# Modulation vectors of a transformer kernel: products on ScalarE and sums by adding DMAs instead of fused multiply-adds on VectorE

## The chip, the cores and the metric

The kernel runs on one core of one Trainium2 chip. The time is the device time of one execution in microseconds (us); the median of three runs is given. The engines are TensorE (PE, with its weight loads as PEld), VectorE (DVE), ScalarE (ACT), GpSimd (POOL) and SyncE (SP, which only issues DMAs here). An engine works through its own queue in order, and waits at an instruction whose semaphores are not yet there.

## The reference, cut to what matters

Two blocks follow each other on 512 tokens of width 1024. The first has two hybrid layers (sliding-window attention, retention, gated linear attention), the second two layers with other mixers and a feed-forward part. All numbers are float32. The change touches the three modulation vectors that each hybrid layer makes from one conditioning vector `c`:

```python
c_act = jax.nn.silu(c)                       # 1 x 1024
mod = c_act @ w_mod + b_mod                  # w_mod 1024 x 3072, per layer
shift, scale, gate = jnp.split(mod[:, None, :], 3, axis=-1)
h = rms_norm(x, pre_gain) * (1.0 + scale) + shift
...
return x + gate * rms_norm(y, post_gain)
```

So each vector is a product of a row of 1024 numbers with a matrix of 1024 x 1024, plus a row of biases; 4 MB of weights are read for each of the six vectors.

## The kernel before, in words

Activations stay in SBUF. Large products run on PE as three passes of float32r matmuls (`mm3`, L230): weights come in tiles of 128 x 512 (`load_w`, L208), SP loads the raw tile (four buffers), ACT casts the high part (L226), DVE subtracts for the low part (L227), and PE uses both. The work of a layer is a set of Python generators (`dsteps`, L328) that are pulled in turn, so that dense matmul steps fill the gaps of the serial parts: the seven levels of the gated attention's decay matrix (`level_ops`, L696, with DVE, ACT and POOL's L704 in turn, and DVE's masked copies L725), the chain of the gated attention (`gla_chain`, L748), the retention (`ret_chain`, L795), the window attention (`attend`, L890).

Modulation vectors: the first layer's first two are made at the very start by other code (`mod0`, L416, on PE and DVE). The other four are made in the background by `mod_steps(l, i)` (L356): layer 0's gate, then layer 1's scale and shift during layer 0, and layer 1's gate during layer 1 (`bg`, L598). They are pulled in the levels (1.5 steps after each of 14 half levels, L722 and L727), then one step for each step of the other chains. A vector has two halves of 512 columns, and a half has eight steps of 128 rows of weights. A step before the change loads a tile `rawm` (two buffers, SP's queue, L368) and does on DVE `acc = rawm * ca[:, k] + acc` (`mod_acc`, L385 to L390; the first step is a product and an addition of the bias row, L387 and L388). The sum over the 128 partitions is left to a matmul with a tile of ones, which gives every partition the result (L375); this part, `late`, is put off by `RT['mdl']` = 4 steps:

```python
ps = ps_mm()
PE.matmul(ps, ones, src, start=True, stop=True)
if i == 0:
    SC.copy(dst, ps)
elif i == 1:
    V.scalar_tensor_tensor(dst, ps, 1.0, dst, op0=OP.add, op1=OP.mult)
else:
    V.tensor_tensor(dst, ps, dst, op=OP.mult)
```

The tile `acc` has one buffer, so a half can begin only when the matmul of the half before has read it. The gain (512 KB, spread over the partitions) is loaded into the vector's own tile ahead (L360), and the late part multiplies by it in place. `later(steps, fn)` (L309) runs `fn` after that many steps of dense matmuls (`tick`, L312); `flush` (L318, called at L686, L792, L881, L1021 and elsewhere) runs at once whatever is still put off. The code gives a program order; the framework then lays out each engine's queue from it and may draw an instruction forward when its operands are there, and it sets all the waits. The layer's gate is read at L1003 and L1005, the next layer's scale and shift at L400 and L401 (`norm`). `bias_steps` (L1109) follows the last vector and uses the same `rawm` buffers.

Of the kernel before, what the change touches and what calls it, by code (L numbers as in the profile page):

```python
# [9 lines left out]
F32 = mybir.dt.float32  # L10
# [4 lines left out]
OP = mybir.AluOpType  # L15
# [6 lines left out]
D = 1024  # L22
# [22 lines left out]
def _constants():  # L45
# [32 lines left out]
    def put2(name, a):  # L78
# [32 lines left out]
RT = dict(f0=5, f1=4, op1=16, op2=6, Lng=7, Le=5, Lc=5, Ld=6, LA=5, LB=5, Lao=5, Lcbn=10, Ldf9=7, Lln=9, Llnf=13, Lrms=7, Lkk=2, Loc=7, Luq=3, Lod=5, h0=17, h1=10,  # L111
          l0=7, lv=3.3, mdl=4, rm=9, na=3, nb=4, u1=4.6, u2=4.4, u0=2.9, df=0.6, cmp=1.485, lr0=0.4, lr1=0.21, lr2=0.175, lr3=0.085, ml=0.5, gl=2, rt=2, at=1, cb=5)
# [9 lines left out]
def _body(ctx, tc, nc, a, out, stop):  # L122
    V, SC, GP, PE = nc.vector, nc.scalar, nc.gpsimd, nc.tensor

    def pool(name, bufs=1, space=None, stack=ctx, side=None):
        kw = {}
        if space:
            kw["space"] = space
        else:
            kw["reuse_waits"] = "tile"  # L130
        if side:
            kw["side"] = side
        return stack.enter_context(tc.tile_pool(name=name, bufs=bufs, **kw))
# [20 lines left out]
    def ps_mm():  # L154
        return psum("mm", [128, 512], 4)
# [26 lines left out]
    ones = cp.tile([128, 128], F32, name="ones")  # L182
# [101 lines left out]
    def bcast_row(dst, row):  # L284
        n = row.shape[-1]
        nc.sync.dma_start(dst, bass.AP(tensor=row.tensor, offset=row.offset, ap=[[0, 128], [1, n]]))
# [22 lines left out]
    def later(steps, fn, key=None):  # L309
        pend.append((clock[0] + steps, fn, key))  # L310
# [31 lines left out]
    def first_block():  # L342
# [3 lines left out]
        md = pool("md", stack=st)  # L346
        more_w("wb", 4, st, None)
        ca = fp.tile([128, 8], F32, name="ca")
# [5 lines left out]
        mod = [[None] * 3 for _ in range(2)]  # L354

        def mod_steps(l, i):  # L356
            t_ = md.tile([128, D], F32, name=f"mod{i}", bufs=1)
            mod[l][i] = t_
            if i:
                bcast_row(t_, (a["pre_norm_gain"] if i == 1 else a["post_norm_gain"])[l])  # L360
            for n in range(0, D, 512):
                c0 = D * i + n
                acc = md.tile([128, 512], F32, name="acc", bufs=1)
                br = md.tile([128, 512], F32, tag="rawm", name="br", bufs=2)[0:1]
                nc.sync.dma_start(br, a["b_mod"][l:l + 1, c0:c0 + 512])
                for k in range(8):
                    raw = md.tile([128, 512], F32, tag="rawm", name="rawm", bufs=2)
                    nc.sync.dma_start(raw, a["w_mod"][l, 128 * k:128 * k + 128, c0:c0 + 512])  # L368
                    mod_acc(acc, raw, br, k)
                    if k < 7:  # L370
                        yield 1

                def late(dst=t_[:, n:n + 512], src=acc):
                    ps = ps_mm()
                    PE.matmul(ps, ones, src, start=True, stop=True)  # L375
                    if i == 0:
                        SC.copy(dst, ps)
                    elif i == 1:
                        V.scalar_tensor_tensor(dst, ps, 1.0, dst, op0=OP.add, op1=OP.mult)
                    else:  # L380
                        V.tensor_tensor(dst, ps, dst, op=OP.mult)
                later(RT['mdl'], late, "mod")
                yield 1

        def mod_acc(acc, raw, br, k, eng=V):  # L385
            if k == 0:
                eng.tensor_scalar(acc, raw, ca[:, 0:1], None, op0=OP.mult)  # L387
                eng.tensor_tensor(acc[0:1], acc[0:1], br, op=OP.add)  # L388
            else:
                eng.scalar_tensor_tensor(acc, raw, ca[:, k:k + 1], acc, op0=OP.mult, op1=OP.add)  # L390

        def norm(l, t, x, pl):
# [5 lines left out]
            for n in range(2):  # L398
# [5 lines left out]
        sil = ([fp.tile([128, 512], F32, name=f"sil_a{t}") for t in range(4)],  # L404
               [fp.tile([128, 256], F32, name=f"sil_r{t}") for t in range(4)])
        Ks = [dict(mod=mod[l], sil=sil, mod_steps=mod_steps, norm=norm, md=md) for l in range(2)]
        load_E, mm_E, ev_E = start_layer(0, Ks[0])
        nst = ExitStack()
# [3 lines left out]
        gain = np_.tile([128, D], F32, name="gain")  # L412
# [1755 lines left out]
```

## Time and profile before

| | before |
|---|---|
| median of three runs | 1942.95 us (1939.66 to 1948.47) |
| the profiled execution's own time | 1936.26 us |
| its span | 1934.5 us |
| mean granted clock of PE | 0.992 |
| busy: PE, DVE, ACT, POOL | 1874.2, 1251.6, 828.1, 260.1 us |
| read from HBM, written | 207.20 MB, 14.09 MB |

The profile is of one execution. A row of instructions gives the source line, the engine, the operation, output and inputs, and shapes; in square brackets stands how long the engine sat idle before it and what ended that wait. A matmul's length overlaps with its neighbours', so a PE that reads as busy is not always at its peak. SP's and POOL's DMA issues appear as instructions; POOL's have a time of their own, since POOL itself writes the transfer's descriptors.

### The profile page before, as it was taken

How to read it: one execution, taken by the hardware profiler on the slowest of the kernel's cores; microseconds unless marked ns; L12 is line 12 of the kernel's file. 1: busy time of each engine (PE TensorE's matmuls, PEld its weight loads, DVE VectorE, ACT ScalarE, POOL GpSimd, SP SyncE). 2: the span in 40 equal slices, each digit the busy share in tenths (PEclk: the TensorE clock that was granted, in tenths of full speed). 3: DMA queues.
4: the chain of work that ended last, by engine and by line, in shares of the span. 5: the costliest groups of instructions: out<-in, count | busy, mean ns of one | idle time of the engine just before them, and what ended most of it. 6: DMA issues, size and time to landing. Idle time of an engine off the chain costs nothing.

```text
span 1934.5 us, 29305 instructions
## 1 busy us (share of the span) xinstructions
PE 1874.2 (97%) x10144; PEld 1518.6 (79%) x10144; DVE 1251.6 (65%) x3060; ACT 828.1 (43%) x1840; POOL 260.1 (13%) x380
## 2 busy tenths in 40 slices
PE   7899899999999999999999999999999999999997
PEld 4777687877888888868888888788778888888886
DVE  5697886485775244686675674755776776756646
ACT  2432354433463344453443443244665544434341
POOL 3011101012101000101020020101441200200101
PEclk9999999999999999999999999999999999999999
DMA  8535524226124233403373362363114033733632
GB/s 278 173 89 165 150 86 137 86 84 183 44 94 157 73 106 121 153 12 116 117 155 99 91 149 72 117 188 91 42 29 148 24 133 112 154 97 96 134 88 82
DMA packets 139784, 218.76 MB, mean 113 GB/s; under 512 B 21633, under 2 KB 53747, under 8 KB 139636
## 3 DMA queue, kind: packets, MB, share of 16 engines
q1 hardware_dynamic: 130420, 200.11, 33.6%
q0 software_dynamic: 9216, 16.78, 5.2%
q8 instruction: 80, 1.31, 0.3%
q14 instruction: 68, 0.56, 0.1%
HBM read 207.20 MB, written 14.09 MB: 114 GB/s over the span
## 4 chain that ended last, share of the span: by engine, by line
PE 65%; DVE 7%; issue 6%; POOL 3%; DMA 2%; ACT 1%; POOLq 0%; DVEq 0%; SPq 0%; ACTq 0%
PE mm L1060 10%; PE mm L1062 10%; PE mm L1061 9%; PE mm L231 6%; PE mm L233 6%; PE mm L232 6%; PE t L1095 1%; PE o L1547 1%; PE o L1549 1%; PE o L1548 1%; DMA bq<-in_ffn_w_down_dram 1%; PE mm L1547 1%; PE mm L1549 1%; PE mm L1548 1%; PE t L274 1%
## 5 line engine op out<-in xcount | busy, mean ns | idle before, releaser
L227 DVE TENSOR_TENSOR w<-raw,w 128x512 fp32r<-128x512 f32 (+4 forms) x496 | 307.5, 638 | 140.1 <-ACT w L226 138.4
L226 ACT CAST w<-raw 128x512 fp32r<-128x512 f32 (+4 forms) x504 | 284.5, 575 | 239.8 <-PE mm L233 55.9
L1060 PE MATMUL mm<-hT,w 128*128 128x512 f32 x920 | 366.6, 399 | 0.2
L1062 PE MATMUL mm<-hT,w 128*128 128x512 f32 x920 | 361.6, 394 | 0.1
L1061 PE MATMUL mm<-hT,w 128*128 128x512 f32 x920 | 360.7, 392 | 0.0
L231 PE MATMUL mm<-w,hT 128*128 128x512 f32 (+3 forms) x704 | 278.3, 396 | 1.4 <-ACT hT L243 1.3
L233 PE MATMUL mm<-w,hT 128*128 128x512 f32 (+3 forms) x704 | 262.5, 373 | 0.4 <-DVE hT L244 0.4
L232 PE MATMUL mm<-w,hT 128*128 128x512 f32 (+3 forms) x704 | 261.0, 371 | 0.1
L1060 PEld LDWEIGHTS mm<-hT,w 128*128 128x128 f32 x920 | 172.9, 188 | 39.7 <-ACT w L226 1.8
L1062 PEld LDWEIGHTS mm<-hT,w 128*128 128x128 f32 x920 | 172.7, 188 | 39.4 <-DVE w L227 1.3
L1061 PEld LDWEIGHTS mm<-hT,w 128*128 128x128 f32 x920 | 172.9, 188 | 35.2
L231 PEld LDWEIGHTS mm<-w,hT 128*128 128x128 f32 x704 | 138.9, 198 | 31.0 <-issue 6.5
L233 PEld LDWEIGHTS mm<-w,hT 128*128 128x128 f32 x704 | 138.8, 197 | 21.9 <-DVE hT L244 1.3
L232 PEld LDWEIGHTS mm<-w,hT 128*128 128x128 f32 x704 | 139.4, 198 | 16.8 <-issue 2.0
L1525 POOL DMA_DIRECT2D bq<-in_ffn_w_down_dram x64 | 56.6, 1280 | 413.0 <-DVE w L244 401.7
L1576 DVE SCALAR_TENSOR_TENSOR g<-mm,cw,g 128x511 f32<-128x511 f32 x44 | 33.0, 749 | 108.5 <-ACT g L1575 108.4
L243 ACT CAST w<-bq 128x512 fp32r<-128x512 f32 x112 | 69.0, 621 | 65.1 <-DMA bq<-in_ffn_w_down_dram 20.2
L1090 ACT ACTIVATE E<-E,nm 128x128 f32<-128x128 f32 (+3 forms) x128 | 71.6, 560 | 45.0 <-DVE nm L1089 42.3
L244 DVE TENSOR_TENSOR w<-bq,w 128x512 fp32r<-128x512 f32 x112 | 75.5, 689 | 15.4 <-ACT w L243 14.8
L1582 DVE TENSOR_TENSOR ge<-ge,mm 128x512 f32<-128x512 f32 x44 | 30.1, 685 | 67.6 <-PE mm L1062 67.5
L1575 ACT ACTIVATE g<-mm,cw 128x512 f32<-128x512 f32 x44 | 34.2, 777 | 79.6 <-PE mm L1062 63.1
L1085 DVE COPY pT<-t 128x512 f32<-128x512 f32 (+3 forms) x84 | 43.0, 512 | 37.8 <-PE t L1280 23.3
(472 smaller groups left out, 3458.3 us busy)
## 6 DMA issues: line engine op xcount, KB each, us to landing
raw<-in_ffn_w_up_dram SPq DMA_DIRECT2D x160, 256.0 KB
rawm<-in_w_mod_dram SPq DMA_DIRECT2D x96, 256.0 KB
raw<-in_w_in_dram SPq DMA_DIRECT2D x80, 256.0 KB
bq<-in_ffn_w_down_dram POOLq DMA_DIRECT2D x64, 256.0 KB, 7.7
raw<-in_ev_w_in_dram SPq DMA_DIRECT2D x48, 256.0 KB
bq<-in_ffn_w_down_dram SPq DMA_DIRECT2D x48, 256.0 KB
raw<-in_w_out_dram SPq DMA_DIRECT2D x32, 256.0 KB
raw<-in_ffn_w_down_dram SPq DMA_DIRECT2D x24, 256.0 KB
```

Of the source, the lines that this page charges most:

```text
L226: SC.copy(hi, r)
L227: (eng or V).tensor_tensor(lo, r, hi.bitcast(F32), op=OP.subtract)
L231: PE.matmul(ps, hi, w[:, 0, w0:w0 + n], start=first, stop=False)
L232: PE.matmul(ps, hi, w[:, 1, w0:w0 + n], start=False, stop=False)
L233: PE.matmul(ps, lo, w[:, 0, w0:w0 + n], start=False, stop=last)
L243: SC.copy(hi, ps)
L244: V.tensor_tensor(lo, ps, hi.bitcast(F32), op=OP.subtract)
L1060: PE.matmul(ps, wh, hi, start=k == ks[0], stop=False)
L1061: PE.matmul(ps, wh, lo, start=False, stop=False)
L1062: PE.matmul(ps, wl, hi, start=False, stop=k == ks[-1])
L1090: SC.activation(E, E, AF.Exp, scale=scale, bias=nm, accum_out=den)
L1525: GP.dma_start(bufs[name, p], src[then](p), accum_op=OP.add)
```

## The change: products on ACT, sums by DMA, one late part for both halves

The loop over the eight tiles of 128 rows is now the outer one and the two halves the inner one, and a step returns to the caller after the load is issued. ACT then multiplies the raw tile by its column of `c`: for the first row tile into the vector's own tile, else in place. The sum is made by DMAs that add to the vector's own tile: the bias row from HBM (2 KB) and each product tile (256 KB). They are issued from POOL. The separate accumulator is gone; its tile name now holds the gain, half by half, loaded inside the late part. The late part covers both halves and is put off by 16 steps instead of 4.

```diff
             t_ = md.tile([128, D], F32, name=f"mod{i}", bufs=1)
             mod[l][i] = t_
-            if i:
-                bcast_row(t_, (a["pre_norm_gain"] if i == 1 else a["post_norm_gain"])[l])
-            for n in range(0, D, 512):
-                c0 = D * i + n
-                acc = md.tile([128, 512], F32, name="acc", bufs=1)
-                br = md.tile([128, 512], F32, tag="rawm", name="br", bufs=2)[0:1]
-                nc.sync.dma_start(br, a["b_mod"][l:l + 1, c0:c0 + 512])
-                for k in range(8):
+            gain = (None, a["pre_norm_gain"], a["post_norm_gain"])[i]
+            for k in range(8):
+                for n in range(0, D, 512):
+                    c0 = D * i + n
+                    acc = t_[:, n:n + 512]
                     raw = md.tile([128, 512], F32, tag="rawm", name="rawm", bufs=2)
                     nc.sync.dma_start(raw, a["w_mod"][l, 128 * k:128 * k + 128, c0:c0 + 512])
-                    mod_acc(acc, raw, br, k)
-                    if k < 7:
-                        yield 1
-
-                def late(dst=t_[:, n:n + 512], src=acc):
+                    yield 1
+                    if k == 0:
+                        SC.mul(acc, raw, ca[:, 0:1])
+                        GP.dma_start(acc[0:1], a["b_mod"][l:l + 1, c0:c0 + 512], accum_op=OP.add)
+                    else:
+                        SC.mul(raw, raw, ca[:, k:k + 1])
+                        GP.dma_start(acc, raw, accum_op=OP.add)
+
+            def late():
+                for n in range(0, D, 512):
+                    dst = t_[:, n:n + 512]
                     ps = ps_mm()
-                    PE.matmul(ps, ones, src, start=True, stop=True)
+                    PE.matmul(ps, ones, dst, start=True, stop=True)
                     if i == 0:
                         SC.copy(dst, ps)
-                    elif i == 1:
-                        V.scalar_tensor_tensor(dst, ps, 1.0, dst, op0=OP.add, op1=OP.mult)
+                        continue
+                    g = md.tile([128, 512], F32, name="acc", bufs=1)
+                    bcast_row(g, gain[l, n:n + 512])
+                    if i == 1:
+                        V.scalar_tensor_tensor(dst, ps, 1.0, g, op0=OP.add, op1=OP.mult)
                     else:
-                        V.tensor_tensor(dst, ps, dst, op=OP.mult)
-                later(RT['mdl'], late, "mod")
-                yield 1
+                        V.tensor_tensor(dst, ps, g, op=OP.mult)
+            later(16, late, "mod")
+            yield 1
```

`mod0`, `mod_acc` and the rest of the kernel stay as they are.

## Rows read from the trace of the kernel before

**Rows 1.** The page's part 1: busy time, share of the span and instructions of each engine.

```profile
PE 1874.2 (97%) x10144; PEld 1518.6 (79%) x10144; DVE 1251.6 (65%) x3060; ACT 828.1 (43%) x1840; POOL 260.1 (13%) x380
```

**Rows 2.** Stretches: length; PE, PEld, DVE, ACT, POOL busy (count); clock, DMA share, GB/s.

```profile
60.00:330.00 270.00, 250.48 (x1541) 203.97 (x1539) 211.02 (x524) 113.35 (x283) 33.58 (x53) 0.99 0.44 131
...
70.00:230.00 160.00, 147.73 (x964) 118.92 (x963) 128.15 (x303) 54.64 (x128) 27.37 (x40) 0.98 0.48 142
100.00:150.00 50.00, 47.66 (x432) 38.65 (x431) 47.12 (x102) 16.73 (x42) 7.79 (x9) 1.00 0.38 109
...
160.00:170.00 10.00, 7.80 (x25) 5.57 (x24) 6.62 (x18) 0.86 (x2) 1.20 (x2) 0.66 0.22 65
...
420.00:430.00 10.00, 9.11 (x120) 8.04 (x117) 9.13 (x20) 3.55 (x8) 2.28 (x2) 0.80 0.39 107
430.00:440.00 10.00, 10.00 (x53) 6.05 (x53) 6.42 (x12) 4.59 (x9) 0.00 (x0) 0.86 0.53 154
```

**Rows 3.** Timeline 72 to 82: start, length, engine, line, operation, [idle before <- what ended it].

```profile
72.88 0.43 SPq L368 DMA_DIRECT2D rawm<-in_w_mod_dram  x1
...
73.83 1.25 SPq L1112 DMA_DIRECT2D tb<-in_rel_bias_dram  x1
...
76.92 0.49 DVE L387 TENSOR_SCALAR acc<-rawm,ca 128x512 f32<-128x512 f32 x1 [4.14 <-DMA rawm<-in_w_mod_dram]
77.43 4.80 SPq L368 DMA_DIRECT2D rawm<-in_w_mod_dram  x4
...
78.26 0.28 PE L617 MATMUL t<-con,ga 128*16 128x128 f32 x1 [1.85 <-DVE ga L612]
...
80.25 1.63 DVE L390 SCALAR_TENSOR_TENSOR acc<-rawm,ca,acc 128x512 f32<-128x512 f32 x2 [2.05 <-DMA rawm<-in_w_mod_dram]
```

**Rows 4.** Timeline, PE at 163 us.

```profile
163.74 2.08 PE L375 MATMUL mm<-acc,ones 128*128 128x512 f32 x2 [1.49 <-DVE acc L390]
```

**Rows 5.** The tile acc: duration min/median/max, first and last start; below, who waited for it.

```profile
L390 DVE SCALAR_TENSOR_TENSOR acc<-rawm,ca,acc x66: 729/750/1673, 6.1 to 428.1; 128x512 f32<-128x512 f32 x66
...
L387 DVE TENSOR_SCALAR acc<-rawm,ca x12: 475/486/1725, 4.9 to 412.9; 128x512 f32<-128x512 f32 x12
L388 DVE TENSOR_TENSOR acc<-acc,br x12: 669/675/680, 5.4 to 413.9; 1x512 f32<-1x512 f32 x12
...
  PEld mm L375: 2.5, 2
  PE mm L375: 2.1, 2
```

**Rows 6.** Groups by line and form, ACT: busy us, mean ns, idle before.

```profile
L1872 ACT ACTIVATE vm<-mm,rk 128x512 f32<-128x512 f32 x4 | 2.8, 690 | 1.5 <-PE mm L233 1.5
```

**Rows 7.** Line L1525, all; then its landings in 960 to 975 and in 990 to 1010.

```profile
L1525 POOL DMA_DIRECT2D bq<-in_ffn_w_down_dram x64: 853/1080/2547, 967.6 to 1803.5; - x64
...
DMA to landing us min/median/max: 3.9/7.7/10.8
...
DMA to landing us min/median/max: 4.5/4.5/4.5
...
DMA to landing us min/median/max: 4.0/8.3/10.8
```

**Rows 8.** Groups by line, POOL, 70 to 235: busy us, mean ns, idle before.

```profile
L704 POOL TENSOR_TENSOR d<-d,kF 128x256 f32<-128x256 f32 x7 | 5.5, 787 | 35.0 <-ACT d L702 17.3 <-PE mm L669 6.7 <-DVE acc L390 6.4
```

**Rows 9.** Lines L1003, L400, L286: duration min/median/max in ns, first and last start.

```profile
L1003 DVE SCALAR_TENSOR_TENSOR sil_a<-sil_a,rstd,mod x8: 746/751/753, 311.5 to 608.2; 128x512 f32<-128x512 f32 x8
...
L400 DVE SCALAR_TENSOR_TENSOR xn<-xo,rstd,mod x8: 745/749/752, 316.5 to 344.0; 128x512 f32<-128x512 f32 x8
...
L286 SPq DMA_DIRECT2D mod<-in_post_norm_gain_dram x2: 328/379/430, 53.0 to 339.7; - x2
```

**Rows 10.** Timeline, DVE: the first half vector's last sum, the second half's first product.

```profile
93.74 0.74 DVE L390 SCALAR_TENSOR_TENSOR acc<-rawm,ca,acc 128x512 f32<-128x512 f32 x1
...
125.43 0.48 DVE L387 TENSOR_SCALAR acc<-rawm,ca 128x512 f32<-128x512 f32 x1
```

## The prediction

> **What bounds the kernel now.** I read the page first, then whole stretches, then single instructions. Over the span TensorE (PE) is busy 97%, VectorE (DVE) 65%, ScalarE (ACT) 43%, GpSimd (POOL) 13% [rows 1]. An average says little here: the four vectors are made between the first load at 72.9 us and the last sum at 428.1 [rows 3, 5], so that part decides, above all its beginning. There PE is not quite full: the stretch from 60 to 330 us leaves 270 − 250.5 = 19.5 us without a matmul, while DVE is busy for 211 of the 270, and for 47 of 50 between 100 and 150 [rows 2]. The worst ten microseconds are 160 to 170: 25 matmuls, where the mean is 1541 / 27 = 57, and a granted clock of 0.66 of 2.4 GHz, a mix of both levels [rows 2].
>
> The reader should see two kinds of stall by the old code. At 76.9 DVE takes a vector's first product after 4.14 us of waiting for its weights; the small copy of L612, which PE needs, stands behind it, and PE waits 1.85 us [rows 3]. At 163.7 PE waits 1.49 us for the last sum of a half vector [rows 4], and the low clock follows. All waits of L375 come to 2.5 + 2.1 = 4.6 us [rows 5]. The rows also show that the queues are not in program order: the rel_bias load of L1112 goes out at 73.83, though its place in the program is a layer later [rows 3]. Vector work is drawn forward to wherever its operands are there.
>
> **What is removed.** Four vectors of 16 tiles: 56 multiply-adds at 750 ns, 8 products at 486 and 8 row additions at 675 [rows 5] (the counts less the 10, 4 and 4 of the first layer's own two vectors, which stay): 42.0 + 3.9 + 5.4 = 51 us of DVE. Most of it lies beside PE work. What can reach the end is only what PE loses: 1.85 us for the ga copy, 4.6 for L375, and the clock after them. For that I count (1 − 0.66) × 7.8 = 2.7 us at 160 to 170, and half of (1 − 0.80) × 9.1 + (1 − 0.86) × 10 = 3.2 at 420 to 440 [rows 2], 1.6. Gain: 1.85 + 4.6 + 4.3 = 11 us. Its bounds are 0 (other waits end at the same moment) and 20 (all of the idle time).
>
> **What is added.** (a) 64 products on ACT. The nearest row is an activation of this shape with a scale from a tile, 690 ns [rows 6]: 64 × 0.69 = 44 us on an engine that is busy 113 of 270 us here [rows 2]. That is free while the weights are there; a product that waits for its load holds up the casts behind it (L226), and with them PE's weights. (b) 56 adding DMAs and 8 adding bias rows on POOL's queue. Issuing a 256 KB DMA there takes 1.08 us (0.85 to 2.55) [rows 7]: 64 × 1.08 = 69 us of POOL, which is busy 34 of 270 us. L704, L281, L282, L775 and L821 stand behind them, and DVE and PE wait for those. If all 14 of L704 in both layers meet one issue, that is 15 us; I take 1, since POOL sat idle for 35 us before seven of them [rows 8]. (c) SP loses the 8 bias rows; its 3 gain loads become 6 half ones, moved into the late step. Their one tile lets the second of a pair start only once DVE has read the first. Bounds 0 and 3 × 2.82 (a load of this size, issued at 77.43, in use at 80.25 [rows 3]) = 8.5; I take 1, as the queues are laid out by readiness. (d) The late step now covers both halves and is asked for 16 steps later, but the flush at L792 cuts that short for the second vector: with 17 steps a vector, 14 pulls of 1.5 in the levels and 13 in the loop of the gated attention make 34 = 2 × 17, so it is asked for at that loop's last pull, and only 32 − 26 = 6 steps of three matmuls lie between. I charge one stall like that of 163.7 with its clock, 1.49 + 2.7 = 4 us, bounds 0 and 4. Costs 1 + 1 + 4 = 6.
>
> No row shows an **adding** DMA. The nearest is the POOL-issued load of the same size: 4.5 us to landing when alone, 7.7 in the median, 3.9 to 10.8 in all [rows 7]. One end is 3.9 (a copy inside the chip may even be shorter), the other 10.8 (it reads two operands). I take 4.5, as the adds come one by one, some 4 us apart, and the row that stood alone is nearest to that. It decides through a loop. A raw tile, one of two, now goes load 2.82, product 0.69, issue and landing 4.5, and load again: 8.0 us for two steps. The 48 steps of the first layer are 24 rounds: 73 + 24 × 8.0 = 265 us. The vectors are first read at 311.5 and 316.5 [rows 9]. So the loop is covered by about 50 us; the second layer's 16 steps, which can start only when the tile is free at 339.7 [rows 9], end near 404, long before their reader.
>
> The Trainium skill ("DMA: Bandwidth & Descriptors", section "Anatomy of one DMA") gives a POOL-issued DMA about 2.0 us plus bytes over 436 GB/s, by estimate 2.6 us for 256 KB. The row that stood alone took 4.5. By the page the loop would end at 73 + 24 × 6.1 = 220, and the slower rival below would have no ground; the sum does not use it.
>
> **Sum.** −11 + 6 = −5 us against the profiled execution's own 1936.26: 1931.3. That execution lay 6.7 below the median 1942.95, so the forecast in medians is **1938**, no change that can be measured: about 0.5%, 9.7 us, is what a measurement of this kernel tells from none.
>
> **Rivals.** *The loop binds: slower.* An add waits on POOL for the product and for the add before it, the product waits on ACT, the reload on SP, and casts, rstd chains and weight loads stand behind them in order. The last vector must have landed by about 313 to serve 316.5. The point from which it decides is (313 − 73) / 24 − 3.5 = 6.5 us to landing. At the median 7.7 the loop ends at 73 + 24 × 11.2 = 342, 29 us late: 1972. At 8.3, the median of the densest stretch [rows 7], it ends at 356, +43: 1986. For it: the landings when several are in flight; DMA engines busy 48% from 70 to 230 before 14.7 MB of adds come on top [rows 2]; and no break any more between halves, where the old single accumulator let the queues catch up from 94 to 125 [rows 10]. Against it: the 4.5 alone.
>
> The Trainium skill ("SBUF — State Buffer", section "SBUF: two separate sides") says that DVE operations in a two-port mode, such as a float32 copy, keep GpSimd from writing the descriptors of its DMAs. If that is what stretched issues to 2.55 us [rows 7], the loop would gain 24 × 1.47 = 35 us and end at 300, in time by 13 us only; no row here parts this cause from others.
>
> *All idle time comes back: faster.* DVE was busy 94% at 100 to 150 [rows 2]; with 51 us gone it never makes PE wait: −20, 1923. For it: the waits named above all end in DVE work. Against it: weight loads share the DMA engines with the adds, and come later rather than earlier.
>
> *It doesn't do what it says.* Products and adds are drawn to other places than the 16 steps suggest, the flushes call the late step at once, and PE sees the same waits under new names: 0, 1943.
>
> **How the numbers follow.** Forecast 0.42, loop 0.30, all idle back 0.22, no effect 0.06. Faster by over 0.5%: 0.22 and a fifth of the forecast's share, 0.30. Slower: 0.30 and a tenth of it, 0.34. Within: 0.36. Cases of both signs hold most of the chance; the forecast's own range, its gain at either bound with the costs as taken, is 1929 to 1949. The range goes from 1921 (1923 with 2 us for the spread of a median) to 1986, the loop at a landing of 8.3 us; beyond it lie longer landings and little else.
>
> **What would show it.** Right: adds landing in under 6 us, the last product of the first layer before 290 us, the L375 waits gone but for one near the flush, the stretch 420 to 440 at full clock. Wrong: ACT's L226 or POOL's L704 and L281 waiting for a rawm load or an add for tens of microseconds, DVE idle before L400, a longer stretch up to 330. A gain past 20 us would mean that DVE, not PE, was the limit of these stretches.

## The result, and the profile after

| | before | after |
|---|---|---|
| median, both on one chip | 1941.31 us (1937.82 to 1948.47, 4 runs) | 1987.11 us (1983.09 to 1990.14, 4 runs) |
| span of the profiled execution | 1934.5 us | 1988.0 us |
| mean granted clock of PE | 0.992 | 0.978 |

The ratio is 1.023 (95% interval 1.021 to 1.025): the changed kernel is 46 us slower. The forecast was no measurable change; the time lies 1 us above the range. In the changed kernel the load is L365, the product L371 (L368 for a vector's first row tile), the adding DMA L372 (L369 for the bias row), the late matmul L378. The code behind `mod_steps` stands six lines lower: old L1003 is L1009, old L704 is L710.

The page of the changed kernel, its parts 1, 5 and 6, answering to [rows 1, 5]:

```profile
PE 1895.5 (95%) x10144; PEld 1537.4 (77%) x10144; DVE 1209.3 (61%) x2988; ACT 865.6 (44%) x1904; POOL 313.5 (16%) x444
...
L371 ACT ACTIVATE rawm<-rawm,ca 128x512 f32<-128x512 f32 x56 | 40.5, 723 | 105.9 <-DMA rawm<-in_w_mod_dram 105.8
L372 POOL DMA_DIRECT2D mod<-rawm x56 | 48.8, 872 | 154.4 <-ACT rawm L371 72.5
...
rawm<-in_w_mod_dram SPq DMA_DIRECT2D x96, 256.0 KB, 3.2
mod<-rawm POOLq DMA_DIRECT2D x56, 256.0 KB, 4.0
```

DVE is busy 1251.6 − 1209.3 = 42 us less (51 had been counted), a product takes 0.72 us and an issue 0.87. What is new stands in the last column of the two middle rows: ACT sat idle for 106 us before products, each time for a load of weights. The list of waits has 44 such waits among the 56 products. A row of that list has the engine, tile and line that waited, what for, the us in all, how often, and the longest; here between 72 and 268 us, the queue of SP's DMA issues (SPq) in the first row:

```profile
SPq L365 <- DMA mod<-rawm: 126.5, 37, 5.4
ACT rawm L371 <- DMA rawm<-in_w_mod_dram: 81.7, 32, 5.4
...
PE o L835 <- DVE ng L559: 6.2, 1, 6.2
PE mm L675 <- POOL d L710: 4.4, 1, 4.4
...
PE mm L232 <- DVE w L227: 0.6, 1, 0.6
```

The load of a raw tile waits for the add that frees it, and the product waits for the load.

Stretches of the changed kernel, to be read against [rows 2] (columns as there):

```profile
60.00:330.00 270.00, 233.34 (x1385) 192.66 (x1384) 151.19 (x418) 125.55 (x293) 68.54 (x89) 0.91 0.59 146
72.50:267.50 195.00, 165.17 (x964) 133.80 (x962) 99.33 (x254) 81.78 (x174) 64.97 (x85) 0.88 0.72 174
160.00:170.00 10.00, 9.56 (x111) 8.34 (x111) 6.80 (x15) 5.46 (x12) 2.79 (x3) 0.91 0.73 174
```

The same matmuls, line by line, in the kernel before, a stretch that was not among its rows (966, since ten of the matmuls with ones fall into it and eight into the other):

```profile
72.00:234.00 162.00, 149.73 (x966) 120.25 (x965) 130.87 (x309) 55.41 (x129) 27.53 (x40) 0.98 0.48 143
```

From 72.5 us on PE needs 195 us for the matmuls that took 162 before: 33 us lost. Idle time is 195 − 165.2 = 29.8 against 162 − 149.7 = 12.3 us, so 17.5 us are new waiting; the other 165.2 − 149.7 = 15.5 are the same matmuls at a mean granted clock of 0.88 in place of 0.98. The readers of the vectors show when it is lost, in line L1009 of the changed kernel (old L1003 of [rows 9]):

```profile
L1009 DVE SCALAR_TENSOR_TENSOR sil_a<-sil_a,rstd,mod x8: 749/752/754, 348.4 to 655.4; 128x512 f32<-128x512 f32 x8
```

The first read comes 348.4 − 311.5 = 36.9 us later, the last, in the second layer, 655.4 − 608.2 = 47.2. The other 6 us of the 53.5 between the two spans lie behind that and are not accounted for.

How a wait for weights reaches PE can be read at two places. The timeline of the changed kernel from 103 to 112 us:

```profile
103.24 0.40 PE L233 MATMUL mm<-w,hT 128*128 128x512 f32 x1
...
103.67 0.72 ACT L371 ACTIVATE rawm<-rawm,ca 128x512 f32<-128x512 f32 x1 [5.30 <-DMA rawm<-in_w_mod_dram]
104.30 0.58 ACT L699 ACTIVATE b<-mm 128x512 f32<-128x512 f32 x1
104.69 0.86 POOL L372 DMA_DIRECT2D mod<-rawm  x1 [5.40 <-ACT rawm L371]
104.90 1.28 ACT L759 ACT_TABLE_LOAD   x1
104.91 0.69 DVE L706 TENSOR_TENSOR d<-b 128x512 f32<-128x512 f32 x1 [3.90 <-ACT b L699]
...
107.12 0.84 POOL L710 TENSOR_TENSOR d<-d,kF 128x256 f32<-128x256 f32 x1 [1.57 <-ACT d L708]
...
108.02 2.66 PE L675 MATMUL mm<-d 32*128 32x128 f32 x16 [4.38 <-POOL d L710]
...
111.20 0.63 PE L232 MATMUL mm<-w,hT 128*128 128x512 f32 x1
```

ACT stands at a product for 5.30 us. Behind it in ACT's queue waits L699, the copy out of PSUM with which a level of the decay matrix goes on; DVE's L706 waits for that copy, POOL's L710 for what follows, and PE 4.38 us for L710. ACT's load of a function table (L759, 1.28 us) stands in that chain too, so not quite all of it is the product's wait. Then the granted clock is down, from 1.00 to 0.50, the lower of its two levels (1.2 of 2.4 GHz): the dense matmuls that took 0.40 us just before the stall take 0.63. The stretches before and after it:

```profile
100.00:104.00 4.00, 3.64 (x17) 2.67 (x16) 0.69 (x1) 0.33 (x1) 0.00 (x0) 1.00 0.57 124
...
110.00:112.00 2.00, 2.00 (x8) 1.54 (x6) 2.00 (x6) 0.72 (x1) 0.82 (x2) 0.50 0.79 158
```

And from 227 to 232 us, the same on POOL:

```profile
227.20 0.72 ACT L371 ACTIVATE rawm<-rawm,ca 128x512 f32<-128x512 f32 x1 [5.03 <-DMA rawm<-in_w_mod_dram]
228.22 0.89 POOL L372 DMA_DIRECT2D mod<-rawm  x1 [4.57 <-ACT rawm L371]
228.87 1.31 POOL L282 TENSOR_TENSOR rs<-rp,mhalf 128x4 f32<-128x4 f32 x1
...
230.21 0.16 DVE L558 TENSOR_TENSOR rs<-rs,con 128x4 f32<-128x4 f32 x1 [6.51 <-POOL rs L282]
...
231.19 0.76 PE L835 MATMUL o<-rsm,rqT 128*128 128x128 f32 x2 [6.22 <-DVE ng L559]
```

POOL's L281 had run at 223.47; its second half, L282, stands behind an add whose product has not been made, and so a root of 512 numbers that PE needs comes five microseconds late.

### The profile page after: what moved, and what is told of

Its sections match the earlier page's. It is cut to its first block, busy times and chain, and to the rows that moved or that the text cites. A ratio compares the mean times of both kernels' runs of the same rounds, so it can differ in the third digit from the quotient of the medians.

```text
span 1988.0 us, 29444 instructions
## 1 busy us (share of the span) xinstructions
PE 1895.5 (95%) x10144; PEld 1537.4 (77%) x10144; DVE 1209.3 (61%) x2988; ACT 865.6 (44%) x1904; POOL 313.5 (16%) x444
## 4 chain that ended last, share of the span: by engine, by line
PE 60%; issue 7%; DVE 6%; DMA 4%; POOL 3%; ACT 2%; SPq 0%; POOLq 0%; DVEq 0%; ACTq 0%
PE mm L1066 9%; PE mm L1068 9%; PE mm L1067 9%; PE mm L231 5%; PE mm L233 5%; PE mm L232 5%; DMA bq<-in_ffn_w_down_dram 2%; PE t L1101 1%; PE o L1553 1%; PE o L1555 1%; PE o L1554 1%; DVE w L227 1%; PE t L274 1%; PE o L1952 1%; PE mm L2022 1%
## 5 line engine op out<-in xcount | busy, mean ns | idle before, releaser
L227 DVE TENSOR_TENSOR w<-raw,w 128x512 fp32r<-128x512 f32 (+4 forms) x496 | 310.4, 644 | 155.0 <-ACT w L226 152.4
L226 ACT CAST w<-raw 128x512 fp32r<-128x512 f32 (+4 forms) x504 | 283.4, 575 | 223.2 <-PE mm L233 45.2
L231 PE MATMUL mm<-w,hT 128*128 128x512 f32 (+3 forms) x704 | 284.2, 404 | 2.4 <-ACT hT L243 1.4
L232 PE MATMUL mm<-w,hT 128*128 128x512 f32 (+3 forms) x704 | 267.4, 380 | 0.8 <-DVE w L227 0.8
L233 PE MATMUL mm<-w,hT 128*128 128x512 f32 (+3 forms) x704 | 267.5, 380 | 0.4 <-DVE hT L244 0.4
L231 PEld LDWEIGHTS mm<-w,hT 128*128 128x128 f32 x704 | 143.8, 204 | 32.7 <-issue 8.4
L233 PEld LDWEIGHTS mm<-w,hT 128*128 128x128 f32 x704 | 143.9, 204 | 21.6 <-DVE hT L244 1.3
L232 PEld LDWEIGHTS mm<-w,hT 128*128 128x128 f32 x704 | 144.7, 206 | 16.4 <-DVE w L227 1.6
L371 ACT ACTIVATE rawm<-rawm,ca 128x512 f32<-128x512 f32 x56 | 40.5, 723 | 105.9 <-DMA rawm<-in_w_mod_dram 105.8
L372 POOL DMA_DIRECT2D mod<-rawm x56 | 48.8, 872 | 154.4 <-ACT rawm L371 72.5
```

What stands on the lines that cost most here:

```text
L226: SC.copy(hi, r)
L227: (eng or V).tensor_tensor(lo, r, hi.bitcast(F32), op=OP.subtract)
L231: PE.matmul(ps, hi, w[:, 0, w0:w0 + n], start=first, stop=False)
L232: PE.matmul(ps, hi, w[:, 1, w0:w0 + n], start=False, stop=False)
L233: PE.matmul(ps, lo, w[:, 0, w0:w0 + n], start=False, stop=last)
```

## Experiments

Three readings were open at the start. By the **hold theory** ("loop theory" in the first four expectations) a raw tile is held too long (through product, issue and landing), and more or freer tiles would mend it. By the **traffic theory** ("cost theory" at first, with a form for ACT's products; later an "issue theory" for POOL's time apart) the added work slows everything: 64 products on ACT, 64 more issues on POOL and 14.7 MB more on the DMA engines. By the **late theory** the loss is in the new order and the late part. A fourth, the **plan theory**, was formed on the way: the queues are laid out when the program is built, and products and adds stand in them ahead of the moment at which their operand lands; whatever stands behind them waits too. Ratios are to the kernel before on the same chip.

### Three raw tiles

```diff
-raw = md.tile([128, 512], F32, tag="rawm", name="rawm", bufs=2)
+raw = md.tile([128, 512], F32, tag="rawm", name="rawm", bufs=3)
...
```

The gain tile goes into the same group of buffers, to make room.

> The changed kernel with three raw tiles instead of two (the gain tile of the late part gives its memory). Loop theory: a product waits on ACT because its raw tile goes round load, product, add in about 8.1 us for two steps, longer than its place in ACT's queue allows; with three tiles a round serves three steps, ACT's 106 us of waiting for raw tiles falls below 60, and the time to 1950 to 1970. Cost theory (the added work itself, 44 us of ACT, 64 issues on POOL, 14.7 MB of adds, takes the time): 1980 or more, since the same work is done. Late theory (outer loop over rows, one late part 16 steps later, gains loaded in it): 1980 or more.

Measured: 1983.72 us, ratio 1.0226 (1.021 to 1.0241). A third tile is worth little: the intervals of two and three tiles overlap, and the hold theory's 1950 to 1970 is missed. The waits of the products are hardly less, and the first layer's last product starts at 263.91 us, where it started at 266.75 with two tiles:

```profile
ACT rawm L371 <- DMA rawm<-in_w_mod_dram: 95.2, 44, 7.6
...
263.91 0.72 ACT L371 ACTIVATE rawm<-rawm,ca 128x512 f32<-128x512 f32 x1 [0.83 <-DMA rawm<-in_w_mod_dram]
```

### No product adds

The sums over the row tiles are left out.

```diff
-GP.dma_start(acc, raw, accum_op=OP.add)
```

> The changed kernel without its 56 adding DMAs of product tiles: the sums over the row tiles are left out, the products on ACT and the loads stay. Loop theory: a raw tile is free at the product's end, a round is 3.2 + 0.7 us as before the change, and the time is 1930 to 1950, with less than 20 us of ACT waiting for raw tiles. Cost theory in its ACT form: 1970 or more, since all 64 products stay on ACT. Cost theory in its POOL and DMA form: 1930 to 1950 as well; the run with three raw tiles parts it from the loop. Late theory: 1980 or more.

Measured: 1929.08 us, ratio 0.994 (0.9925 to 0.9954), 11 us below the 1940.09 of before. Without the adds the products on ACT leave no loss, so the traffic theory in its form for ACT falls. ACT still waits 37.8 us for weights, and that costs nothing here: not every such wait reaches PE (the list of waits, then the stretches):

```profile
ACT rawm L371 <- DMA rawm<-in_w_mod_dram: 37.8, 28, 4.2
```

```profile
60.00:330.00 270.00, 254.40 (x1567) 209.77 (x1566) 177.89 (x476) 145.79 (x340) 40.71 (x64) 0.98 0.42 129
```

So the adds cost about 1987 − 1929 = 58 us, one way or another (by the ratios 0.029 of the time, 56 us).

### Products on DVE, adds as they are

```diff
-SC.mul(raw, raw, ca[:, k:k + 1])
+V.tensor_scalar(raw, raw, ca[:, k:k + 1], None, op0=OP.mult)
...
```

> The changed kernel with its products on DVE (0.49 us each, in place) instead of ACT, the adds by DMA as they are. Loop theory: the wait goes along with the product, DVE waits 70 to 110 us for raw tiles, and the time stays at 1965 to 2005. Cost theory in its ACT form: ACT is free of 44 us and of the waits, below 1955.

Measured: 1972.91 us, ratio 1.0176 (1.0151 to 1.0202). ACT is clear of the vectors, and 34 us of the loss remain: the waiting goes to DVE and POOL. The time is in the range of the hold theory; DVE's waits for raw tiles, 51.5 us, are below the 70 to 110 that it gave.

```profile
POOL mod L372 <- DVE rawm L371: 109.9, 38, 9.1
DVE rawm L371 <- DMA rawm<-in_w_mod_dram: 51.5, 29, 5.1
```

### Sums on DVE, in the new order and with the new late part

```diff
-SC.mul(raw, raw, ca[:, k:k + 1])
-GP.dma_start(acc, raw, accum_op=OP.add)
+V.scalar_tensor_tensor(acc, raw, ca[:, k:k + 1], acc, op0=OP.mult, op1=OP.add)
...
```

> The changed loop order, the one late part after 16 steps and the gains loaded in it, but products and sums on DVE as before the change (fused multiply-add into the vector's own tile; only the bias row is added by DMA). Loop theory: no add holds a raw tile, so 1925 to 1950. Late theory: the slow-down is in this part, 1970 or more.

Measured: 1930.35 us, ratio 0.9961 (0.994 to 0.9983), faster than before, so the late theory falls. What is left of the change is its order of steps, the sum in the vector's own tile, the bias rows added by DMA, and the late part 16 steps later with its gains; DVE keeps nearly all of its work (205.58 us of the 270, with 211.02 before):

```profile
60.00:330.00 270.00, 254.40 (x1566) 209.82 (x1565) 205.58 (x519) 116.70 (x291) 44.40 (x63) 0.98 0.42 129
330.00:480.00 150.00, 147.02 (x980) 117.43 (x978) 102.58 (x246) 55.50 (x124) 26.21 (x36) 1.00 0.41 125
```

The intervals of this run and of the run without adds overlap: nearly the same gain comes with DVE's work in place. Whether the freed DVE time is worth something that the products on ACT take away again, these two runs don't tell.

### Five raw tiles

As with three, with `bufs=5`; one of the four weight tiles is given up for the room.

> The changed kernel with five raw tiles (one weight tile of four in the pool wb and the gain tile give the memory). Three tiles did not help, which leaves two readings. Hold theory (a fixed number of tiles is held too long, and three were too few): with five, a product's load is five steps ahead, ACT's wait for raw tiles goes below 40 us and the time below 1960. Plan theory (each engine's queue is laid out for adds shorter than the chip's; more tiles only let the layout pack products closer, until the add of the same half two steps before is what binds): 1970 or more, with ACT or POOL still waiting 60 us or more for raw tiles or adds.

Measured: 1979.21 us, ratio 1.0191 (1.0167 to 1.0215). The plan theory's range held, the hold theory's (under 1960 us, waits under 40) did not. With tiles in plenty the products still stand and wait, and POOL's adds now wait for the add before to the same columns:

```profile
ACT rawm L371 <- DMA rawm<-in_w_mod_dram: 79.6, 41, 7.2
POOL mod L372 <- DMA mod<-rawm: 23.1, 14, 3.7
```

### Adds from HBM

The adds take unscaled weights from HBM; the products stay and are not used.

```diff
-GP.dma_start(acc, raw, accum_op=OP.add)
+GP.dma_start(acc, a["w_mod"][l, 128 * k:128 * k + 128, c0:c0 + 512], accum_op=OP.add)
```

> The changed kernel, but the adding DMAs take the unscaled weights from HBM as their source and not the product tile (the sum is then over unscaled weights from the second row tile on); the products stay and are not used. POOL issues, bytes added and the order of the adds are those of the changed kernel, and HBM is read for 14.7 MB more; only the raw tile is free at the product's end. Hold and plan theory: below 1955, ACT's wait for raw tiles below 40 us. Traffic and issue theory (POOL's 64 issues and the DMA engines' load): 1970 or more.

Measured: 1983.3 us, ratio 1.0215 (1.0192 to 1.0239). The raw tile is now free when the product ends, and the last product of the first layer came at 213.2 instead of 266.8 us; the time did not move. Hold and plan theory had both been given less than 1955 us here, and both missed; the range of the traffic and issue theory, 1970 or more, held. The run is not the clean cut that it was meant to be: an add now lands in 5.5 us where it took 4.0, and a load of weights in 4.2 where it took 3.2. So it shows that an earlier end of the loop alone brings nothing, and that the wait went to another place, in front of the adds on POOL:

```profile
POOL mod L372 <- DMA mod<-in_w_mod_dram: 101.1, 45, 5.4
ACT rawm L371 <- DMA rawm<-in_w_mod_dram: 73.1, 38, 6.2
...
213.21 0.72 ACT L371 ACTIVATE rawm<-rawm,ca 128x512 f32<-128x512 f32 x1 [3.09 <-DMA rawm<-in_w_mod_dram]
...
DMA to landing us min/median/max: 4.2/5.5/8.0
```

### Tiny adds

The adds take 4 of 512 columns; the rest of the sum is left out.

```diff
-GP.dma_start(acc, raw, accum_op=OP.add)
+GP.dma_start(acc[:, 0:4], raw[:, 0:4], accum_op=OP.add)
```

> The changed kernel with its adding DMAs cut to 4 of 512 columns (the rest of the sum is left out): traffic nearly gone, 56 issues on POOL and the hold of the raw tile stay, the hold shorter, some 2 to 3 us instead of 4. Hold theory: 1940 to 1965. Traffic theory: as with no adds, 1925 to 1938. Issue theory (POOL's time): 1970 or more.

Measured: 1953.41 us, ratio 1.0059 (1.004 to 1.0077). The issues and the program's order are those of the changed kernel, the traffic is nearly gone, and ACT's waits for loads fell from 105.8 to 68.3 us (in an execution of 1943.99 us, the fastest of nine). Line L372 of this run:

```profile
DMA to landing us min/median/max: 2.0/2.5/5.9
```

The landing is 1.5 us shorter; over 24 rounds of two steps that is 36 us, and 0.0171 × 1941 = 33 us came back. The time lies in the hold theory's range and above the traffic theory's (1925 to 1938), but this run alone does not part a shorter landing from less traffic.

### Sums on DVE with three raw tiles

The kernel with sums on DVE, `bufs=3`.

> The version with products and sums on DVE in the new loop order and one late part (1930.35), with three raw tiles instead of two. All theories: 1920 to 1935, as its raw tiles are held by DVE alone; the loads run one step further ahead, which may save the 17 us that DVE waited for them in part.

Measured: 1931.9 us, ratio 0.9951 (0.993 to 0.9972): the same as with two.

### Steps drawn evenly, with and without ordering edges

Both kernels start from the one with five raw tiles. The vector steps are drawn from `tick`, one for every four dense matmul steps, and no longer in the levels. One of the two also gives every product and every add an ordering edge to the dense matmul ahead of it in the program; the edge asks for no semaphore, it only tells the framework in which order to lay out the queues:

```diff
+def behind(i):
+    if GATE:
+        tc.add_manual_dep(i.ins, lastmm[0].ins.name,
+                          mybir.DependencyInfo(mybir.DependencyClass.NoSync, mybir.DependencyReason.DATA), reason="gate")
...
+        if hook[0] is not None:
+            hook[1] -= 1
+            if hook[1] <= 0:
+                hook[1] = GAP
+                next(hook[0], None)
...
-SC.mul(raw, raw, ca[:, k:k + 1])
-GP.dma_start(acc, raw, accum_op=OP.add)
+behind(SC.mul(raw, raw, ca[:, k:k + 1]))
+behind(GP.dma_start(acc, raw, accum_op=OP.add))
```

> The changed kernel with five raw tiles (the kernel with three weight tiles of that run), and two things more: one vector step is drawn after every four dense matmul steps in place of the pulls in the levels, and each product and each add carries an ordering edge to the dense matmul before it in the program, so that it can't be laid into its engine's queue ahead of that place. Amount of work, adds and traffic are unchanged. Plan theory (an instruction that stands in an in-order queue before its operand has landed holds up what is behind it): ACT's waits for raw tiles (79.6 us with five tiles) and POOL's for the add before (23.1 us) fall under half, and the time is under 1950 us. Traffic theory (64 more issues on POOL and 14.7 MB more on the DMA engines slow everything): 1970 us or more, with the waits spread over other loads.

> The same without the ordering edges: the steps are drawn as evenly in the program, but the queues are free to lay products and adds ahead. Plan theory: most of the stalls are back, since the queues pack them as closely as the planned landing allows: 1965 us or more, waits for raw tiles above 60 us. If the even drawing alone were what matters: within 5 us of the kernel with the edges. Traffic theory: the same time as with the edges, both at 1970 or more.

Measured with the edges: 1949.35 us, ratio 1.0045 (1.0019 to 1.0072). Without: 1977.88 us, ratio 1.0198 (1.0157 to 1.0239). The programs differ by the edges alone, the times by 28 us. Waits and stretch of the kernel without edges:

```profile
ACT rawm L387 <- DMA rawm<-in_w_mod_dram: 77.3, 41, 4.6
POOL mod L388 <- DMA mod<-rawm: 34.9, 15, 6.2
```

```profile
60.00:330.00 270.00, 241.90 (x1438) 198.45 (x1438) 157.42 (x435) 134.20 (x311) 67.77 (x89) 0.91 0.60 152
```

And of the kernel with edges:

```profile
POOL mod L388 <- ACT rawm L387: 87.5, 29, 8.2
```

```profile
60.00:330.00 270.00, 254.73 (x1566) 211.06 (x1565) 176.88 (x474) 144.48 (x338) 77.73 (x105) 0.97 0.66 172
...
330.00:480.00 150.00, 144.99 (x917) 116.15 (x916) 86.59 (x208) 62.27 (x132) 34.04 (x43) 0.94 0.54 144
```

The readers of the gate vectors in both (first and last start), with edges, then without:

```profile
L1025 DVE SCALAR_TENSOR_TENSOR sil_a<-sil_a,rstd,mod x8: 746/752/754, 303.5 to 609.7; 128x512 f32<-128x512 f32 x8
...
L1025 DVE SCALAR_TENSOR_TENSOR sil_a<-sil_a,rstd,mod x8: 747/752/754, 337.7 to 643.9; 128x512 f32<-128x512 f32 x8
```

With edges no product waits for its load any more. PE makes 1566 matmuls from 60 to 330 us, more than the 1541 of [rows 2], while the DMA engines are busier (0.66) than in the changed kernel (0.59). The first read comes at 303.5 us, earlier than the 311.5 of before, although the first layer's last product starts only at 286.07. So the traffic theory falls for the loss in the first layer: the same issues and the same bytes are there, and it is gone. POOL does still wait for products (87.5 us). What stays of the loss lies later: from 330 to 480 us PE makes 917 matmuls where the run with sums on DVE made 980. From the first read to the last, 306.2 us pass with the edges and 306.2 without; before the change it was 608.2 − 311.5 = 296.7. The edges gave the first layer back and did nothing for the second.

### The same pacing, sums on DVE

> The kernel with the sums on DVE in the new order and the late step 16 steps later (1930 us), now with the vector steps drawn after every four dense matmul steps and the ordering edges on the sums. Plan theory: DVE's waits for raw tiles (16.6 us) go to under 5 us, and the time is 1920 to 1932. Traffic theory: no difference beyond 3 us from the kernel without pacing, since there are no adding DMAs to slow anything.

Measured: 1931.29 us, ratio 0.9965 (0.9947 to 0.9982). DVE's waits for raw tiles are gone from the list, and the time is that of the kernel without pacing. Where the sums stay on DVE, pacing and edges are worth nothing that can be measured. From the first read to the last, 296.8 us pass:

```profile
L1024 DVE SCALAR_TENSOR_TENSOR sil_a<-sil_a,rstd,mod x8: 747/751/753, 306.7 to 603.5; 128x512 f32<-128x512 f32 x8
```

### Pacing and edges with two raw tiles

The kernel with the edges, with two raw and four weight tiles.

> The paced kernel with the ordering edges, but with two raw tiles and four weight tiles as in the changed kernel. Plan theory in its strict form (only the places in the queues matter, not the number of tiles): the time stays within 8 us of the paced kernel with five raw tiles, 1941 to 1957. Loop theory (a pair of tiles cannot turn in less than 8.1 us, so products come late wherever they stand): the steps are drawn about as fast as that loop, so ACT's waits for raw tiles are back at 60 us or more in the first layer, and the time is 1965 or more.

Measured: 1961.79 us, ratio 1.0111 (1.0079 to 1.0144), between the two expectations. The steps are drawn about as fast as a pair of tiles can turn, and some of the waits are back:

```profile
ACT rawm L387 <- DMA rawm<-in_w_mod_dram: 37.3, 20, 6.1
```

Both readings missed in part: the time is above the one's 1957 and below the other's 1965, and the waits are under 60 us. At two tiles, pacing and edges bring the ratio from 1.023 to 1.0111, about half of the loss. In the first layer they bring back more: the first read comes at 318.2 us, 30 us before the changed kernel's and 7 behind the one of before.

```profile
L1025 DVE SCALAR_TENSOR_TENSOR sil_a<-sil_a,rstd,mod x8: 745/753/754, 318.2 to 622.0; 128x512 f32<-128x512 f32 x8
```

The number of tiles matters once the places in the queues are right: 0.0066 × 1938 = 13 us between two and five, which were worth 0.0039 in the changed kernel's order.

**A version that beats both.** Three kernels with the sums on DVE, in the new order and with the late part put off by 16 steps, ran at 0.9961, 0.9951 and 0.9965 of the kernel before, each interval below 1: some 8 us faster, without a single adding DMA for the products. Each difference alone is within the half per cent named ahead; the three agree.

## Why the prediction was wrong

**The step that failed** is the sentence "So the loop is covered by about 50 us", and with it "That is free while the weights are there" in the cost of the products, which put the waits for weights at nothing. The size of the loop was right: adds landed in 4.0 us (3.3 to 6.8) where 4.5 was taken, a round of two steps took 8.1 us on average where 8.0 was worked out, the last product of the first layer began at 266.75 where 265 was given. That the end fits to 2 us is partly luck: a third tile, with which a round would serve three steps, moved it only to 263.91. And the slack was measured at the wrong reader. The reader of the finished vector at 311.5 had 50 us to spare; at the two places shown, the work that stands behind a product in ACT's queue, and behind an add in POOL's, had none. With two tiles a product waits for a load that itself waits for an add; from 72.5 to 267.5 us ACT stood so for 81.7 us in 32 waits of up to 5.4, and PE lost 33 us there, 17.5 of them in new waiting and 15.5 at the lower clock. By the prediction's own point of decision, 6.5 us to landing, a landing of 4.0 was safe; the kernel became 46 us slower. That places in the queues make the first layer's loss is shown by the pair that differs in the edges alone (28 us); for the second layer it is not shown.

**The slower rival** was near in time (1972 to 1986 for 1987.11), by luck in part, and its mechanism was half right. Product on ACT, add on POOL, reload on SP wait in turn, as it says. It put the price at the end of the loop, though, and expected casts (L226) and weight loads to be what is held up. Between 72 and 268 us PE's list of waits has 0.6 us for a tile of weights (L227) in the changed kernel; it waits for the levels' L710, for the roots of L282, for the gated attention's copies. Two runs show the difference: with adds from HBM the loop ended 54 us earlier, at the same time for the whole; with edges and five tiles it ended 19 us later, and the kernel was 36 us faster (0.0185 of the time).

**The gain of 11 us** was near in size (11.0 in the run without adds), but its sum counts two waits twice: the 2.5 us of L375's weight loads and the 2.1 of its matmuls are the same two stalls, so the sum is 1.85 + 2.1 + 4.3 = 8. Its source was not shown. The prediction gave it to DVE's freed 51 us; with the sums back on DVE the gain is 8 us by the ratio (10 by the medians) all the same. It can be had from what is left in that run: the order of the halves, the sum in the vector's own tile, the bias rows by DMA, the later late part. Which of them earns it was not tried.

**The small costs.** (b) An issue took 0.87 us, not 1.08. POOL's L710 sat idle for less than L704 had in both layers (26.1 us after ACT's L708 against 51.1 after L702), yet PE now waits 5.6 us for it: one microsecond was too little. (c) The gain tiles: DVE waited once, 5.0 us, for a gain at L385, PE 1.0 us; 1 was right. (d) The late part: L378 stood idle for 1.4 us in all; 4 was too much.

**The landing and the issues.** An add landed in 4.0 us in the median, and the row of the kernel before, 4.5, was near. The Trainium skill ("DMA: Bandwidth & Descriptors", section "Anatomy of one DMA") gave by estimate 2.6 us. A shorter landing would not have saved the forecast: with the tiny adds, at 2.5 us, the kernel still took 1953 us. The issues of the adds took 850 to 932 ns. By the Trainium skill ("SBUF — State Buffer", section "SBUF: two separate sides") DVE might have stretched them; nothing of that shows here.

**What stays open.** With edges and five tiles 0.0105 of the time, 20 us, still lies between the kernel and the run without adds. Between the first layer's reader and the second's 306.2 us pass, with and without edges, 9.4 more than in the run with sums on DVE and the same pacing (296.8). With the tiny adds that part took 295.6 us (318.1 to 613.7), so in the second layer the size of the adds seems to matter, through their landing or their traffic; the two were not parted there. The rest lies behind the second layer's reader and is unexplained. Whether another pacing would close it was not tried.

## What to carry to other kernels

When a step is moved onto an in-order engine, price its wait by what stands right behind it in that queue, and not by the slack of whoever reads its result in the end. Here a chain through several engines (load, product, add, load) became cheaper where each link was placed behind the moment at which its operand lands, and it took an explicit order in the queues to hold it there. Part the gain before crediting it: here a gain of the forecast's size came with nearly all of the work left on DVE.

## What the runs showed of the hardware

A DMA that adds 256 KB into another tile lands in 4.0 us (3.3 to 6.8), where a plain load of that size in the same run took 3.2; cut to 16 bytes in each partition it still takes 2.5. Reading its addend from HBM, it took 5.5 (4.2 to 8.0). The loads of the vectors' weights (L365) hardly suffered from the adds: 3.2 us in the median with them, 3.1 in the run without; with adds from HBM they took 4.2. And a stall cost PE more than its length: after the one of 4.38 us the granted clock was 0.50, and about half of the 33 us lost in the first layer was matmuls at a lower granted clock.
